# A second feed-forward product by seven products instead of eight, in three parts of its inner dimension

## The chip, the cores and the metric

The kernel runs on one core of a Trainium2 chip. The metric is the time of one execution on the device, in microseconds (us); a kernel is run several times and the median counts. One further execution is taken with the hardware profiler, and the rows below come from it. Its engines are TensorE (PE; its weight loads are PEld), VectorE (DVE), ScalarE (ACT), GpSimd (POOL) and SyncE (SP), whose queue issues nearly all DMAs.

## The reference

One layer of a streaming encoder on `x` of 2048 x 1024, all in float32. The mixer sub-layer (convolution, gated recurrence and chunked attention side by side) comes first and is not touched. What matters here is the second sub-layer:

```python
h = x * (1.0 + sc2) + sh2
gt, up = jnp.split(h @ w_ffn_in[l], 2, axis=-1)      # 2048 x 1024 @ 1024 x 5632
y = (jax.nn.silu(gt) * up) @ w_ffn_out[l]            # 2048 x 2816 @ 2816 x 1024
x = layer_norm(ALPHA * x + (1.0 + g2) * y, ln2_g[l], ln2_b[l])
```

The second feed-forward product is the one with `w_ffn_out`, of inner dimension 2816, which is 22 slabs of 128.

## The kernel before

The program's instructions are emitted in program order with priorities (`shifted(tc, -BOOST)` takes a block ahead by 2000), and the framework's own timeline then fixes the order of each engine's queue. It takes work far ahead where buffers are free. Each queue is worked off in order.

Every float32 product is made of three passes. An operand is split into a rounded high part and a low rest (`split_hl`, L828: a cast on ScalarE, L829, and a subtraction on VectorE, L830), and `PASSES` multiplies high by high, high by low and low by high. One matmul takes a stationary block of 128 x 128 and a moving one of 128 x 512.

The first feed-forward product (`ffn_in`, L943) already works by a seven-product scheme. Its inner dimension of 1024 is taken in two halves of `NK` = 4 slabs, its tokens in two rounds `g` of 1024, each in two blocks of 512. `load_ops` (L868) loads the moving operands of a round, seven combinations of four slabs, from DRAM into 28 pairs of tiles (`oph`, `opl`) through raw buffers of the tag `h2`, six deep. `load_fi` (L904) loads the weights of slab `f` into `fraw`, forms the seven stationary combinations with four GpSimd operations (L930, L931, L933, L937) and splits each into `fhi` and `flo`. The loop over `f` (22 slabs) then makes 84 matmuls per slab in four PSUM banks (L953), adds on VectorE while they drain (L958), applies SiLU, multiplies (L986) and writes the slab's 1024 tokens to DRAM (`actd`). Weights of slab `f+1` are loaded while `f` is multiplied.

The second product (`ffn_out`, L1022) is plain. It takes the 1024 output columns in two halves `dh` of 512. For each it loads 22 weight slabs as moving operands (`wo`, raw buffers `wraw`, five deep) and the rows `ga`, `ba` (the first norm's scale and shift times ALPHA) and `g2`. Tokens go in blocks of four tiles of 128, the last four in two blocks of two. For each block the activations come back from DRAM (`araw`), are split (`ahi`, `alo`) and multiplied (`mul`, L1095): 22 slabs x 3 passes into one bank per tile. `fetch` loads the residual row (L1043), scales it on ScalarE (L1045) and on GpSimd (L1046, L1047); `evac` multiplies the bank by `g2` (L1116), adds (L1117) and takes the statistics (L1111). The first half's rows wait in DRAM (`zh`); in the second half `norm_out` (L1050) normalizes a tile (L1065 to L1067) and stores it. The very last tile is multiplied in two column halves of 256 and ends in four steps on VectorE (L1060, L1062).

Of the kernel before, what the change touches and what calls it, by code (L numbers as in the profile page):

```python
# [38 lines left out]
N_H2 = 6  # L39
LN2 = 0.6931471805599453  # L40
# [792 lines left out]
def ffn_open(tc, env):  # L833
    pf = env["pf"] = ExitStack()
    env["p1"] = pf.enter_context(tc.tile_pool(name="p1", bufs=1, side="right", reuse_waits="tile"))
    st = env["st_es"] = ExitStack()
    env["st"] = st.enter_context(tc.tile_pool(name="st", bufs=1, side="right", reuse_waits="tile"))
    env["actd"] = [tc.dram_tile([P, NG * 2 * Q], F32, name=f"actd{f}") for f in range(NF)]
    env["ops"] = load_ops(tc, env, 0, range(2))
# [64 lines left out]
def load_fi(tc, env, f, first=False):  # L904
    nc, pw = tc.nc, env["pw"]
    ops = []
# [14 lines left out]

    def op(src):
        hi = pw.tile([P, NK, P], F32R, name="fhi", tag="fhi", bufs=N_WOP)
        lo = pw.tile([P, NK, P], F32R, name="flo", tag="flo", bufs=N_WOP)
        split_hl(nc, src, hi, lo)
        ops.append((hi, lo))
# [15 lines left out]

def ffn_in(tc, env, g, f, w, ops):  # L943
    nc, pw = tc.nc, env["pw"]

    def bank():
        k = "pj" if f % 2 else "pm"
        return env[k].tile([P, Q], F32, name="pi", tag=k)

    def prod(out, n, first):  # L950
        for idx in range(NK):
            for i, (a, c) in enumerate(PASSES):
                nc.tensor.matmul(out=out, lhsT=w[n][a][:, idx, :], rhs=ops[n, idx][c],  # L953
                                 start=first and idx == 0 and i == 0, stop=idx == NK - 1 and i == 2,
                                 skip_group_check=not first)
# [31 lines left out]
    nc.sync.dma_start(out=env["actd"][f][:, g * 2 * Q:(g + 1) * 2 * Q], in_=s.rearrange("p a b -> p (a b)"))  # L987


def ffn_phase(tc, env):  # L990
# [11 lines left out]
    for g in range(NG):  # L1002
        for f in range(NF):
# [18 lines left out]
def ffn_out(tc, env, p2):  # L1022
    nc = tc.nc
    rows, w_fo, out = (env[k] for k in ("rows", "w_fo", "out"))
    epsc, NQ, pw = env["epsc"], env["NQ"], env["pw"]
    NT = NQ * NB
    zh = tc.dram_tile([NT, P, 512], F32, name="zh")
    st2 = p2.tile([P, NT, 2, 6], F32, name="st2")
    st4 = p2.tile([P, 4, 6], F32, name="st4")
    mv = p2.tile([P, NT, 2], F32, name="mv2")  # L1030
    rs = p2.tile([P, NT, 2], F32, name="rs2")

    def row_half(i, dh, tag, bufs=1):
        t = p2.tile([P, 512], F32, name="row", tag=tag, bufs=bufs)
        nc.sync.dma_start(out=t, in_=rows[i, dh * 512:dh * 512 + 512].partition_broadcast(P))
        return t

    def residual(t, dh, ga, ba):
        q, tt = t // NB, t % NB
        sc, nb = env["norms"][q]  # L1040
        ry = pw.tile([P, 2, 512], F32, name="res", tag="fu", bufs=N_U)
        r = ry[:, 0]
        nc.sync.dma_start(out=r.rearrange("p (b c) -> p b c", b=2),  # L1043
                          in_=env["zall"][q * 4 + 2 * dh:q * 4 + 2 * dh + 2, :, tt, :].rearrange("b p c -> p b c"))
        nc.scalar.activation(out=r, in_=r, func=AF.Identity, scale=sc[:, tt:tt + 1], bias=nb[:, tt:tt + 1])  # L1045
        nc.gpsimd.tensor_tensor(out=r, in0=r, in1=ga, op=ALU.mult)  # L1046
        nc.gpsimd.tensor_tensor(out=r, in0=r, in1=ba, op=ALU.add)  # L1047
        return r, ry[:, 1]

    def norm_out(t, z0, z1, lg, lb):  # L1050
        nc.vector.bn_aggr(out=mv[:, t, :], in_=st4 if t == NT - 1 else st2[:, t])
        nc.scalar.activation(out=rs[:, t, 0:1], in_=mv[:, t, 1:2], func=AF.Sqrt, bias=epsc[:, 0:1])
        nc.vector.reciprocal(out=rs[:, t, 0:1], in_=rs[:, t, 0:1])
        last = t == NT - 1
        if not last:
            nc.vector.scalar_tensor_tensor(out=rs[:, t, 1:2], in0=mv[:, t, 0:1], scalar=-1.0, in1=rs[:, t, 0:1],
                                           op0=ALU.mult, op1=ALU.mult)
        for dh, z in enumerate((z0, z1)):
            if last:
                nc.vector.scalar_tensor_tensor(out=z, in0=z, scalar=mv[:, t, 0:1], in1=lg[dh],  # L1060
                                               op0=ALU.subtract, op1=ALU.mult)
                nc.vector.scalar_tensor_tensor(out=z, in0=z, scalar=rs[:, t, 0:1], in1=lb[dh],  # L1062
                                               op0=ALU.mult, op1=ALU.add)
            else:
                nc.scalar.activation(out=z, in_=z, func=AF.Identity, scale=rs[:, t, 0:1], bias=rs[:, t, 1:2])  # L1065
                nc.vector.tensor_tensor(out=z, in0=z, in1=lg[dh], op=ALU.mult)
                nc.vector.tensor_tensor(out=z, in0=z, in1=lb[dh], op=ALU.add)  # L1067
            nc.sync.dma_start(out=out[t * P:(t + 1) * P, dh * 512:dh * 512 + 512], in_=z)

    lg = lb = None  # L1070
    for dh in range(2):
        blocks = [range(4 * i, 4 * i + 4) for i in range(4)]
        if dh:
            blocks = blocks[:3] + [range(12, 14), range(14, 16)]
        with shifted(tc, -BOOST):
            wo = [load_op(tc, env, w_fo[f * P:(f + 1) * P, dh * 512:dh * 512 + 512], f % NK, p2, "wraw", 5)
                  for f in range(NF)]
            ga, ba, g2 = (row_half(i, dh, f"row{i}") for i in (R_LN1G, R_LN1B, R_G2))
            nc.sync.dma_start(out=g2, in_=env["g2d"][:, dh * 512:dh * 512 + 512])
            for r in (ga, ba):  # L1080
                nc.vector.tensor_scalar(out=r, in0=r, scalar1=ALPHA, scalar2=None, op0=ALU.mult)
            if dh:
                lg = [row_half(R_LN2G, i, "rowlg", 2) for i in range(2)]
                lb = [row_half(R_LN2B, i, "rowlb", 2) for i in range(2)]
        for bi, ts in enumerate(blocks):
            k = "pj" if bi % 2 else "pm"
            n = len(ts)
            pts = [env[k].tile([P, 512], F32, name="po", tag=k) for _ in ts]
            tail = ts[-1] == NT - 1 and n == 2
            zr, parts = {}, {}  # L1090

            def mul(f, j, c=slice(0, 512)):
# [122 lines left out]
```

## Time and profile before

| | us |
|---|---|
| median of 3 runs | 2602.72 |
| lowest and highest | 2598.47, 2602.81 |
| the profiled execution | 2589.91 |
| its span, first to last instruction | 2588.2 |
| first product, first to last matmul start | 1227.0 to 2094.7 |
| second product, first to last matmul start | 2086.0 to 2580.2 |

The two products overlap by some 8 us, since the first matmuls of the second one stand between the last ones of the first. A busy TensorE counts from the start of a matmul to its modelled end, and matmuls overlap; how many are started in a stretch tells more than the mean duration.

### The profile page before, as it was taken

Reading aid. Unit: us, or ns where it says so; the run is one execution under the profiler, and the core shown is the slowest. Engines: PE = TensorE matmul, PEld = TensorE weight load, DVE = VectorE, ACT = ScalarE, POOL = GpSimd, SP = SyncE. Lnnn points to the kernel's source line nnn. Section 1 sums busy time; section 2 is a strip of 40 time slices with the busy share of each in tenths; the row PEclk is TensorE's granted clock in tenths of the full one; section 3 lists DMA queues with packets and bytes.
Section 4 is the critical chain, followed back from the end, with each engine's and each line's share of the span. In section 5 each row is a group of like instructions: output and inputs, shape, how many; then the busy total and the mean of one; then the engine's idle time right before and its main releaser. Section 6 shows DMA issues by size and latency. Waiting matters only on the chain.

```text
span 2588.2 us, 36360 instructions
## 1 busy us (share of the span) xinstructions
PE 2457.8 (95%) x13274; PEld 2078.5 (80%) x13274; DVE 1656.1 (64%) x2917; ACT 997.2 (39%) x1920; POOL 665.7 (26%) x571
## 2 busy tenths in 40 slices
PE   6888899999999999987999999999999999999998
PEld 5766799879977898876878788888888888888887
DVE  7987696669557785666655555765445474364666
ACT  2444444354244433544323333433333352242333
POOL 3433112200152112510333332332322211111121
PEclk8997999999999999988999999999999999999999
DMA  9676667663755645547333332442222274454544
GB/s 354 212 236 187 186 197 264 201 180 128 241 183 172 205 164 184 191 135 259 102 117 119 118 130 90 164 142 91 74 82 90 74 244 142 130 182 134 161 147 142
DMA packets 202691, 423.99 MB, mean 164 GB/s; under 512 B 20240, under 2 KB 69008, under 8 KB 202512
## 3 DMA queue, kind: packets, MB, share of 16 engines
q1 hardware_dynamic: 202352, 421.15, 49.8%
q8 instruction: 104, 1.70, 0.3%
q14 instruction: 75, 0.61, 0.1%
q0 software_dynamic: 160, 0.52, 0.1%
HBM read 317.78 MB, written 95.42 MB: 160 GB/s over the span
## 4 chain that ended last, share of the span: by engine, by line
PE 78%; DVE 10%; DMA 6%; issue 3%; ACT 2%; POOL 1%; SPq 0%; DVEq 0%; POOLq 0%; ACTq 0%
PE pi L953 31%; PE po L1095 17%; PE pjt L270 11%; PE pjt L321 9%; PE lp L513 2%; DVE cacc L377 2%; PE sc L625 1%; PE tp L661 1%; PE tp L648 1%; DMA whl<-wki 1%; DMA whl<-wko 1%; PE lp L533 1%; DMA xst<-zall 1%; DMA opraw<-srcd 1%; DMA xb<-in_x_dram 1%
## 5 line engine op out<-in xcount | busy, mean ns | idle before, releaser
L953 PE MATMUL pi<-oph,fhi 128*128 128x512 f32 x1232 | 484.1, 393 | 17.8 <-ACT fhi L829 11.9
L953 PE MATMUL pi<-opl,fhi 128*128 128x512 f32 x1232 | 483.7, 393 | 0.0
L953 PE MATMUL pi<-oph,flo 128*128 128x512 f32 x1232 | 478.9, 394 | 0.0
L270 PE MATMUL pjt<-hh,whl 128*128 128x512 f32 x1184 | 402.5, 411 | 16.2 <-DMA whl<-wki 6.4
L953 PEld LDWEIGHTS pi<-oph,fhi 128*128 128x128 f32 x1232 | 232.4, 189 | 70.2 <-ACT fhi L829 12.1
L829 ACT CAST fhi<-fraw 128x512 fp32r<-128x512 f32 x220 | 136.2, 621 | 392.3 <-PE pi L953 376.6
L270 PEld LDWEIGHTS pjt<-hh,whl 128*128 128x128 f32 x1184 | 227.4, 194 | 66.4 <-DMA whl<-wki 6.0
L958 DVE TENSOR_TENSOR fu<-fu,pi 128x512 f32<-128x512 f32 x176 | 120.8, 686 | 245.8 <-PE pi L953 245.1
L953 PEld LDWEIGHTS pi<-opl,fhi 128*128 128x128 f32 x1232 | 232.5, 189 | 52.3
L1095 PE MATMUL po<-oph,alo 128*128 128x512 f32 (+1 forms) x702 | 273.9, 390 | 0.0
L1095 PE MATMUL po<-oph,ahi 128*128 128x512 f32 (+1 forms) x702 | 270.1, 385 | 3.1 <-DVE res L1116 3.1
L1095 PE MATMUL po<-opl,ahi 128*128 128x512 f32 (+1 forms) x702 | 272.6, 388 | 0.0
L953 PEld LDWEIGHTS pi<-oph,flo 128*128 128x128 f32 x1232 | 232.3, 189 | 49.5 <-DVE flo L830 0.2
L830 DVE TENSOR_TENSOR alo<-araw,ahi 128x512 fp32r<-128x512 f32 x172 | 148.5, 871 | 190.9 <-ACT ahi L829 174.3
L270 PE MATMUL pjt<-hl,whl 128*128 128x512 f32 x592 | 243.0, 411 | 0.0
L321 PE MATMUL pjt<-whl,yh 128*128 128x256 f32 x1024 | 196.7, 288 | 15.5 <-DMA whl<-wko 12.0
L830 DVE TENSOR_TENSOR flo<-fraw,fhi 128x512 fp32r<-128x512 f32 x220 | 159.5, 742 | 70.9 <-ACT fhi L829 70.8
L377 DVE SCALAR_TENSOR_TENSOR cacc<-u,cs,cacc 128x512 f32<-128x512 f32 x240 | 195.3, 843 | 0.2
L829 ACT CAST ahi<-araw 128x512 fp32r<-128x512 f32 x172 | 104.9, 618 | 222.3 <-PE po L1095 208.0
L321 PEld LDWEIGHTS pjt<-whl,yh 128*128 128x128 f32 x1024 | 164.1, 194 | 17.7 <-DVE yl L231 7.9
L930 POOL TENSOR_TENSOR ft<-fraw 128x512 f32<-128x512 f32 x43 | 59.9, 1392 | 450.6 <-DMA fraw<-in_w_fi_dram 433.5
L1095 PEld LDWEIGHTS po<-oph,ahi 128*128 128x128 f32 x702 | 132.4, 189 | 31.7 <-DVE res L1116 3.3
(257 smaller groups left out, 4539.1 us busy)
## 6 DMA issues: line engine op xcount, KB each, us to landing
whl<-wki SPq DMA_DIRECT2D x156, 512.0 KB, 3.8
fraw<-in_w_fi_dram SPq DMA_DIRECT2D x86, 512.0 KB, 3.7
araw<-actd SPq DMA_DIRECT2D x154, 256.0 KB, 3.4
wki<-whl SPq DMA_DIRECT2D x52, 512.0 KB, 4.3
whl<-wko SPq DMA_DIRECT2D x48, 512.0 KB, 3.5
actd<-fs SPq DMA_DIRECT2D x44, 512.0 KB, 3.3
xb<-in_w_ada_dram SPq DMA_DIRECT2D x64, 256.0 KB, 4.7
opraw<-srcd SPq DMA_DIRECT2D x56, 256.0 KB, 5.0
```

Source lines behind the costliest of these rows:

```text
L270: nc.tensor.matmul(out=ps[j], lhsT=w[kt // 2][a][:, kt % 2, j * P:(j + 1) * P], rhs=hts[kt][c], start=(kt == 0 and n == 0), stop=(kt == KT ...
L321: nc.tensor.matmul(out=ps[tt // 2][:, tt % 2, :], lhsT=lhs[2 * kp + k][c][:, tt * P:(tt + 1) * P], rhs=w[kp][a][:, k, :], start=(ko == 0 a ...
L377: nc.vector.scalar_tensor_tensor(out=ac, in0=us[j][:, t:t + Q], scalar=col(wc + t), in1=ac, op0=ALU.mult, op1=ALU.add)
L513: nc.tensor.matmul(out=lp[0:n, c, :], lhsT=ddf[:, c * P:c * P + n], rhs=d4[:, c, :, :], start=True, stop=True)
L533: nc.tensor.matmul(out=lp[:, c, :], lhsT=K[:, 2 * i + c, :], rhs=M[:, 2 * i + c, :], start=True, stop=True)
L625: nc.tensor.matmul(out=sc[:, 0:n + x], lhsT=qs[hd][ph][:, i * P:(i + 1) * P], rhs=kt_[:, o - x0:o - x0 + n + x], start=ph == 0, stop=ph == 1)
L829: nc.scalar.copy(out=hi, in_=src)
L830: nc.vector.tensor_tensor(out=lo, in0=src, in1=hi.bitcast(F32), op=ALU.subtract)
L930: e.tensor_tensor(out=t1, in0=w12, in1=w11, op=ALU.subtract)
L953: nc.tensor.matmul(out=out, lhsT=w[n][a][:, idx, :], rhs=ops[n, idx][c], start=first and idx == 0 and i == 0, stop=idx == NK - 1 and i == ...
L958: nc.vector.tensor_tensor(out=out, in0=a, in1=b, op=ALU.add)
L1095: nc.tensor.matmul(out=pts[j][:, c], lhsT=a[x][:, j * P:(j + 1) * P], rhs=wo[f][y][:, c], start=f == 0 and m == 0, stop=f == NF - 1 and m ...
```

## The change

The second product goes by the same seven-product scheme as the first. Two token tiles of 128 are the halves of the stationary side, two column halves of 512 those of the moving side, and the inner slabs are taken in pairs: 11 pairs. Seven operands of all 11 pairs don't fit in the 28 pairs of tiles, so the pairs are taken in three parts of 4, 3 and 4 (`PARTS`). Each part goes over all tokens in 8 units of two tiles. Between parts the two 1024-wide rows of a unit go to DRAM (`zp`) and come back.

- `wo_part`, called 11 times in the second round of the first product: loads a pair of weight slabs in four blocks, multiplies them by `g2` (four GpSimd operations), forms the combinations (four more) and writes seven operands to DRAM (`wsrc`). That is 8 GpSimd operations and 11 DMAs of 256 KB each time. It uses the tiles of `st` (`h2`, `h2s`, `xst`).
- `stationary` is the second half of `load_fi`, now for `n` slabs; `products` is the bank and matmul code of `ffn_in`, now for `nk` slabs.
- `ffn_out` is new; `row_half`, `residual`, `norm_out` and the block loop go. `g2` is no longer multiplied there.

```diff
+PARTS = ((0, 4), (4, 3), (7, 4))
...
+def wo_part(tc, env, p):
...
+            nc.sync.dma_start(out=t, in_=env["w_fo"][(2 * p + k) * P:(2 * p + k + 1) * P, h * 512:h * 512 + 512])
+            e.tensor_tensor(out=t, in0=t, in1=env["g2r"][h], op=ALU.mult)
...
+    e.tensor_tensor(out=s1, in0=a21, in1=a22, op=ALU.add)
+    e.tensor_tensor(out=s2, in0=s1, in1=a11, op=ALU.subtract)
+    e.tensor_tensor(out=s3, in0=a11, in1=a21, op=ALU.subtract)
+    e.tensor_tensor(out=s4, in0=a12, in1=s2, op=ALU.subtract)
+    for n, src in enumerate((a11, s2, s3, a12, s1, a22, s4)):
+        nc.sync.dma_start(out=env["wsrc"][p][n], in_=src)
...
+            if g == 1 and f >= 2 and f % 2 == 0:
+                wo_part(tc, env, f // 2 - 1)
+            if g == 1 and f == NF - 1:
+                wo_part(tc, env, NF // 2 - 1)
...
+    def load_ops(part):
+        p0, n = PARTS[part]
+        return {(m, i): load_op(tc, env, env["wsrc"][p0 + i][m], i, p2, "wraw", 4)
+                for m in range(7) for i in range(n)}
+
+    def load_a(part, u):
...
+        a = [pw.tile([P, NK, 2 * P], F32, name="araw", tag="fraw", bufs=N_RAW) for _ in range(2)]
...
+        return stationary(tc, env, a[0][:, 0:n, 0:P], a[1][:, 0:n, 0:P], a[0][:, 0:n, P:], a[1][:, 0:n, P:], t1, t2)
+
+    def load_z(part, t, ga, ba):
+        r = pw.tile([P, 2, 512], F32, name="zr", tag="fu", bufs=N_U)
+        rf = r.rearrange("p a c -> p (a c)")
+        if part:
+            nc.sync.dma_start(out=rf, in_=zp[t])
+            return r
...
+        nc.scalar.activation(out=rf, in_=rf, func=AF.Identity, scale=sc[:, tt:tt + 1], bias=nb[:, tt:tt + 1])
+        nc.vector.tensor_tensor(out=rf, in0=rf, in1=ga, op=ALU.mult)
+        nc.gpsimd.tensor_tensor(out=rf, in0=rf, in1=ba, op=ALU.add)
+        return r
+
+    def close(part, t, r, lg, lb):
...
+        if part < 2:
+            nc.sync.dma_start(out=zp[t], in_=rf)
+            return
...
+        if t < NT - 2:
...
+            nc.scalar.activation(out=rf, in_=rf, func=AF.Identity, scale=sd, bias=nb)
+            nc.vector.tensor_tensor(out=rf, in0=rf, in1=lg, op=ALU.mult)
+            nc.gpsimd.tensor_tensor(out=rf, in0=rf, in1=lb, op=ALU.add)
+            nc.sync.dma_start(out=out[t * P:(t + 1) * P, :], in_=rf)
+            return
+        for c in (slice(512, D), slice(0, 512)):
+            nc.vector.scalar_tensor_tensor(out=rf[:, c], in0=rf[:, c], scalar=mv[:, t, 0:1], in1=lg[:, c],
...
+    def add(o, b, part, t=None, c=0):
         with shifted(tc, -BOOST):
...
+            nc.vector.tensor_tensor(out=o, in0=o, in1=b, op=ALU.add)
+            if part == 2 and t is not None:
+                nc.vector.bn_stats(out=st2[:, t, c, :], in_=o)
+
+    def unit(part, u, w, ops, z):
...
+        ba, bb = bank(), bank()
+        prod(ba, 0, True)
+        prod(bb, 1, True)
+        with shifted(tc, -BOOST):
+            nc.scalar.copy(out=v, in_=ba)
+        add(v, bb, part)
+        with shifted(tc, -BOOST):
+            for o in (y[:, 1], x[:, 1], y[:, 0]):
+                nc.gpsimd.tensor_tensor(out=o, in0=o, in1=v, op=ALU.add)
+        bc = bank()
+        prod(bc, 2, True)
+        add(y[:, 1], bc, part)
+        prod(ba, 3, False)
+        add(x[:, 0], ba, part, t, 0)
+        bd = bank()
+        prod(bd, 4, True)
+        add(y[:, 1], bd, part, t + 1, 1)
+        prod(bc, 5, False)
+        add(x[:, 1], bc, part, t, 1)
+        prod(bd, 6, False)
+        add(y[:, 0], bd, part, t + 1, 0)
...
+    for i, (part, u) in enumerate(steps):
+        if u == 0:
+            with shifted(tc, -BOOST):
...
+                ops = load_ops(part)
+        z = [load_z(part, 2 * u + k, ga, ba) for k in range(2)]
+        cur = w
+        if i + 1 < len(steps):
+            w = load_a(*steps[i + 1])
+        unit(part, u, cur, ops, z)
+        for k in range(2):
+            close(part, 2 * u + k, z[k], lg, lb)
```

The rows of a unit use four buffers (`fu`, two units), its raw activations four (`fraw`), the split weights seven pairs (`fhi`, `flo`), as in the first product.

## Rows read from the trace of the kernel before

**Rows 1.** The page, its first part: busy time of each engine, share, instructions.

```profile
PE 2457.8 (95%) x13274; PEld 2078.5 (80%) x13274; DVE 1656.1 (64%) x2917; ACT 997.2 (39%) x1920; POOL 665.7 (26%) x571
```

**Rows 2.** Windows: stretch, length, busy PE, PEld, DVE, ACT, POOL; PEclk, DMA share, GB/s.

```profile
1650.00:1700.00 50.00, 50.00 (x219) 40.67 (x218) 45.64 (x62) 28.18 (x52) 14.87 (x8) 1.00 0.80 259
...
1800.00:1900.00 100.00, 100.00 (x439) 82.05 (x438) 48.02 (x67) 31.56 (x53) 28.00 (x20) 1.00 0.24 81
...
2100.00:2200.00 100.00, 100.00 (x438) 82.07 (x437) 49.31 (x62) 31.31 (x51) 18.22 (x12) 1.00 0.54 172
2200.00:2300.00 100.00, 100.00 (x438) 82.06 (x437) 51.44 (x67) 32.63 (x53) 24.84 (x16) 1.00 0.50 156
```

**Rows 3.** TensorE's waits from 1250 us on: total us, times, longest.

```profile
PE pi L953 <- DVE fu L958: 5.4, 3, 2.4
PE po L1095 <- DVE res L1116: 3.1, 1, 3.1
```

**Rows 4.** Groups by form, one of the three passes: full and half-width matmuls.

```profile
L1095 PE MATMUL po<-oph,ahi 128*128 128x512 f32 x674 | 261.5, 388 | 0.0
...
L1095 PE MATMUL po<-oph,ahi 128*128 128x256 f32 x28 | 8.6, 306 | 3.1 <-DVE res L1116 3.1
```

**Rows 5.** The chain that ended last, pieces of the stage's beginning and end.

```profile
2086.43 1.60 PE po L1095 x7
2088.03 2.75 PE pi L953 x12
...
2571.17 9.35 PE po L1095 x66
```

**Rows 6.** Groups by form on VectorE, 1227 to 2589 us.

```profile
L830 DVE TENSOR_TENSOR flo<-fraw,fhi 128x512 fp32r<-128x512 f32 x220 | 159.5, 742 | 70.9 <-ACT fhi L829 70.8
...
L986 DVE TENSOR_TENSOR fs<-fs,fu 128x1024 f32<-128x1024 f32 x44 | 53.7, 1220 | 0.0
```

**Rows 7.** A group of GpSimd's weight combinations.

```profile
L933 POOL TENSOR_TENSOR fraw<-fraw 128x512 f32<-128x512 f32 x43 | 69.5, 1616 | 3.0
```

**Rows 8.** Timeline of GpSimd in two stretches: start us, us, operation.

```profile
1664.55 1.69 POOL L937 TENSOR_TENSOR fraw<-fraw,ft 128x512 f32<-128x512 f32 x1 [1.83 <-DVE flo L830]
1666.32 1.62 POOL L931 TENSOR_TENSOR ft<-fraw,ft 128x512 f32<-128x512 f32 x1
...
1907.76 1.30 POOL L930 TENSOR_TENSOR ft<-fraw 128x512 f32<-128x512 f32 x1 [12.38 <-DMA fraw<-in_w_fi_dram]
1909.13 1.63 POOL L933 TENSOR_TENSOR fraw<-fraw 128x512 f32<-128x512 f32 x1
```

**Rows 9.** Timeline of VectorE in the same stretches.

```profile
1664.40 4.09 DVE L830 TENSOR_TENSOR opl<-opraw,oph 128x512 fp32r<-128x512 f32 x3
...
1907.94 0.69 DVE L958 TENSOR_TENSOR fu<-fu,pi 128x512 f32<-128x512 f32 x1 [1.39 <-PE pi L953]
1908.54 1.06 DVE L830 TENSOR_TENSOR flo<-fraw,fhi 128x512 fp32r<-128x512 f32 x1
1911.16 0.69 DVE L830 TENSOR_TENSOR flo<-fraw,fhi 128x512 fp32r<-128x512 f32 x1 [1.55 <-ACT fhi L829]
```

**Rows 10.** Waits of all engines, 1225 to 2589 us: total us, times, longest.

```profile
ACT fhi L829 <- PE pi L953: 515.6, 277, 6.6
POOL ft L930 <- DMA fraw<-in_w_fi_dram: 433.5, 38, 14.1
...
POOL fraw L937 <- DVE flo L830: 80.3, 41, 16.6
```

**Rows 11.** SP's issues of operand loads (start, us), and the DMA table's line for them.

```profile
1655.67 18.58 SPq L862 DMA_DIRECT2D opraw<-srcd  x17
...
opraw<-srcd SPq DMA_DIRECT2D x56, 256.0 KB, 5.0
```

**Rows 12.** Windows of 3 us at the last block's wait, columns as in rows 2.

```profile
2570.00:2573.00 3.00, 1.83 (x8) 1.84 (x9) 1.96 (x5) 0.00 (x0) 0.00 (x0) 0.60 0.47 175
2573.00:2576.00 3.00, 3.00 (x24) 3.00 (x23) 0.00 (x0) 0.00 (x0) 0.00 (x0) 0.84 0.00 0
```

More of the change, by code (lines that the diff above doesn't have):

```diff
@@ L905, in load_fi @@
     nc, pw = tc.nc, env["pw"]
-    ops = []
     if first:
@@ L940, in load_fi, with products, bank, prod @@
     return ops
+def wo_part(tc, env, p):
+    nc, st = tc.nc, env["st"]
+    e = nc.gpsimd
+    if p == 0:
+        env["g2r"] = [st.tile([P, 512], F32, name="g2r", tag="xst", bufs=3) for _ in range(2)]
+        for h, t in enumerate(env["g2r"]):
+            nc.sync.dma_start(out=t, in_=env["g2d"][:, h * 512:h * 512 + 512])
+    a = {}
+    for k in range(2):
+        for h in range(2):
+            t = a[k, h] = st.tile([P, 512], F32, name="wos", tag="h2", bufs=N_H2)
+            nc.sync.dma_start(out=t, in_=env["w_fo"][(2 * p + k) * P:(2 * p + k + 1) * P, h * 512:h * 512 + 512])
+            e.tensor_tensor(out=t, in0=t, in1=env["g2r"][h], op=ALU.mult)
+    a11, a21, a12, a22 = a[0, 0], a[0, 1], a[1, 0], a[1, 1]
+    s1, s2, s3, s4 = (st.tile([P, 512], F32, name="wos", tag="h2s", bufs=4) for _ in range(4))
+    e.tensor_tensor(out=s1, in0=a21, in1=a22, op=ALU.add)
[4 more added lines that the diff above has]
+        nc.sync.dma_start(out=env["wsrc"][p][n], in_=src)
+def products(tc, env, i, w, ops, nk):
+    nc = tc.nc
+    def bank():
+        k = "pj" if i % 2 else "pm"
+        return env[k].tile([P, Q], F32, name="pi", tag=k)
+    def prod(out, n, first):
+        for idx in range(nk):
+            for j, (a, c) in enumerate(PASSES):
+                nc.tensor.matmul(out=out, lhsT=w[n][a][:, idx, :], rhs=ops[n, idx][c],
+                                 start=first and idx == 0 and j == 0, stop=idx == nk - 1 and j == 2,
+                                 skip_group_check=not first)
+    return bank, prod
 def ffn_in(tc, env, g, f, w, ops):
     nc, pw = tc.nc, env["pw"]
[L946 to L955, printed above, removed]
+    bank, prod = products(tc, env, f, w, ops, NK)
     def add(out, a, b):
@@ L1023, in ffn_out @@
     nc = tc.nc
[L1024 removed]
+    rows, out = env["rows"], env["out"]
     epsc, NQ, pw = env["epsc"], env["NQ"], env["pw"]
     NT = NQ * NB
[L1027 to L1029 removed]
+    zp = [tc.dram_tile([P, D], F32, name=f"zp{t}") for t in range(NT)]
     mv = p2.tile([P, NT, 2], F32, name="mv2")
     rs = p2.tile([P, NT, 2], F32, name="rs2")
[L1033 to L1036 removed]
@@ L1045, in residual @@
[L1045 to L1056, printed above, removed]
-                                           op0=ALU.mult, op1=ALU.mult)
[L1058 to L1068, printed above, removed]
@@ new lines, in ffn_out @@
+    lg = lb = ga = ba = None
+    nu = NT // 2
+    steps = [(part, u) for part in range(3) for u in range(nu)]
+    w = load_a(0, 0)
+    for i, (part, u) in enumerate(steps):
+        if u == 0:
+            with shifted(tc, -BOOST):
+                if part == 0:
+                    ga, ba = row(R_LN1G), row(R_LN1B)
+                    for r in (ga, ba):
+                        nc.vector.tensor_scalar(out=r, in0=r, scalar1=ALPHA, scalar2=None, op0=ALU.mult)
+                if part == 2:
+                    lg, lb = row(R_LN2G), row(R_LN2B)
+                ops = load_ops(part)
[4 more added lines that the diff above has]
+        unit(part, u, cur, ops, z)
+        for k in range(2):
+            close(part, 2 * u + k, z[k], lg, lb)
```

134 lines of the change are left out of this document (36 added, 98 removed).

## The prediction

> **What bounds the kernel now.** The page's busy shares come first: TensorE holds 95% of the span, VectorE 64%, GpSimd 26% [rows 1]. Busy PE alone proves little, so the second view is the table by stretches: in the stage that is rewritten TensorE is busy in all of 2100 to 2300, at the full granted clock (2.4 GHz), and starts 438 matmuls in each 100 us, one per 0.2283 us (84 in a second-product unit: 19.18 us); VectorE is half busy, GpSimd a fifth [rows 2]. The third view is TensorE's waits: after 1250 us there are 8.5 us of them in all, 3.1 of these in the last block [rows 3]. So the stage is bound by the number of matmuls; a matmul removed is worth 0.2283 us, so long as everything else keeps under TensorE's pace. The question is what that "so long as" costs.
>
> **1. Matmuls.** Before, 2 halves x 16 tiles x 22 slabs x 3 passes = 2112, the last tile's second 66 split into two of 256 columns [rows 4]: 2046 full ones x 0.2283 = 467.1, and 132 halves at 9.35/66 = 0.1417 us [rows 5] = 18.7; with the 3.1 us wait, 488.9. The chain agrees: 2086.43 to 2580.51, less the two interleaved pieces of the first product, is 488.6 [rows 5]. After, 7 products x 3 passes x (4+3+4) x 8 units = 1848 x 0.2283 = 421.9. Gain 67.0, the ceiling.
>
> **2. The port in the steady units.** An uncontended 512-wide GpSimd add takes 1.30 us, the next starts 0.07 later; the timelines then show it and VectorE taking turns. A VectorE subtraction with both inputs in SBUF that starts inside a GpSimd add takes 1.06 us instead of the 0.69 of its neighbour, ending 0.54 after that add; the GpSimd add behind it takes 1.63. Three `opl` subtractions beside two adds need 4.09 us [rows 8, 9]. An add from PSUM meanwhile keeps its 0.69. So two-SBUF VectorE work and GpSimd work exclude each other; an add holds the port for 1.16 us (the second one ends that long after the subtraction does, 1910.76 less 1909.60) and a subtraction for about 0.55. The Trainium skill is of two minds. Its GPSIMD Engine Reference, § Specifications, names instructions with two SBUF inputs among those that contend, as the rows do; Advanced Engine Details and Errata, § VectorE Performance Modes, lets only the two-port modes block GpSimd and gives `tensor_tensor` none, by which the 13 us below would be nothing and the sum 39 instead of 26. The rows here decide for the first.
> A full unit of part 0 or 2 gives GpSimd seven 512-wide adds (four for the next weights, three of `v`) and two 1024-wide ones. No row shows a 1024-wide one: between 2.3 us (two port times) and 3.2 (two contended ones); I take 2 x 1.30, the least that one alone takes, twice. It meets seven subtractions, each costing it 0.33, and two 1024-wide VectorE multiplies, 0.9 each (their row is 1.22, next start 0.09 earlier [rows 6]). Sum 7 x 1.37 + 2 x 2.67 + 7 x 0.33 + 2 x 0.9 = 19.0 us, against TensorE's 19.18: level. VectorE, at 0.60 a slot [rows 9], does in part 2 seven subtractions, six PSUM adds, four statistics, two multiplies of 1.13 and about 0.8 of small work: 13.3, and about nine waits of 0.7 for the port: 19.6, just over. In part 0 it is 10.1 + 6.3. Part 1 is lighter in all (three slabs, no wide adds): GpSimd about 10 of 14.4 us. Units next to a part's border have no wide adds either, so six units in each of parts 0 and 2 are heavy. With a queue this full, some waits reach TensorE: I take 0.6 us per unit in part 0 and 1.5 in part 2: 4 + 9 = 13 us. Bounds: 0, as in the first product's second round, where GpSimd is 28% busy (1800 to 1900 [rows 2]) and TensorE never waits, and 59 (rival B). I am nearer to the first, since the sums come out level with TensorE and not above.
>
> **3. The three operand loads.** Each part needs 7 x n operand pairs (28, 21, 28), loaded, cast and subtracted while the last unit before still uses the slots. Before has one like it, at 1650 to 1700: VectorE 45.6 of 50 us busy, DMA share 0.80 at 259 GB/s, and no wait on TensorE [rows 2, 3]. Its cover was six raw buffers and little GpSimd work: 17 issues in 18.58 us, 1.09 us per operand, landing in 5.0 [rows 11]. Four buffers stretch that to 1.64. Into part 0: last first-product unit and first new unit hold, in port time, 16.5 (weights for the next unit, the SiLU product, two rows of `z`) and 18.9 (a full unit: 7 x 1.16 + 2 x 2.4 + 7 x 0.55 + 2 x 1.08), and 28 x 0.55 = 15.4: 50.8 in 38.4 us, 12 late. Into part 1: two light units of 9.8 and 21 x 0.55, 31.2 in 33.6, 17 raws past the prefetched four at 1.64 = 28 us before the last is needed at 32.9: I take 2. Into part 2: two units of 12.0 and 15.4, 39.3 in 33.6, 6 late by the port; by bytes, 28 operands of 0.26 MB and two units' own 2.9 and 3.1 MB make 13.3 MB, 41 us at 259/0.80 GB/s, 7 late; the buffers give 6. Together I take 9. Sum 23 us; bounds 0 (the load of before) and 40 (each cause adds to the others). Waits of this size also lower the clock: after the 3.1 us wait the granted clock is 0.60 and 0.84 over the next two 3 us stretches, part of each at the lower level of 1.2 GHz [rows 12], about 1.3 us lost; three times 4 us, rounded for late restarts: 4.
>
> **4. What is hidden, and its cover.** `wo_part` adds 88 GpSimd operations to the second round of the first product, 13 us per two units that already hold 11 of 38 us, and 121 DMAs on SP's queue, in order before the weight loads. TensorE's 100% covers them; GpSimd mostly waits for those loads there, and ACT waits for TensorE [rows 10]. If a store stuck in SP's queue held a weight load for longer than its unit of slack, the whole lateness would show. Partial rows add 2 MB per unit, in and out: with operands 3 MB per 19.18 us = 157 GB/s against 156 to 172 now [rows 2]. In part 1 it is 2.75 MB in 14.4 us, 191, still under 259. A row's reload two units ahead waits for its store; four row buffers leave some 8 us. ACT, at 31% in the stage [rows 2], gets one copy and two row scalings per unit. Cost 0; if that cover goes, the late row delays `y`'s add, then the bank of product 5.
>
> **5. Tail.** After the last matmul, before: 256-wide add, add, statistics, then four 512-wide steps (L1116, L1117, L1109, L1060, L1062), the out store. After: one 512-wide add and statistics less the multiply, but the neighbour tile's closing stands on VectorE as well: +1 us, from 0 to +2.
>
> **Sum.** 67 - 13 - 23 - 4 - 1 = 26 us gained. The profiled execution took 2589.91 (span 2588.2 and 1.7 around it), 12.8 below the median of the runs, 2602.72; I take the gain off each: 2564 for a profile like that one, 2577 for the median. A difference within 0.2%, 5 us, is no difference that a measurement of this kernel can tell.
>
> **Rivals.** A: port and loads stay covered, as at 1650 to 1700. For it: the sums of step 2 lie level with TensorE, and late work can be taken ahead in part 1; against: a full port has no slack and [rows 8, 9] show the exclusion. Then only byte-limited lateness (7), clock (1) and tail (1) remain: gain 58, 2545. Chance 0.2.
> B, slower: GpSimd becomes the bound. The adds of `v` stand in its in-order queue among weight adds that wait for VectorE's subtractions (80.3 us over 41 units now, 2 us each [rows 10]); `y`'s add waits for it, VectorE's queue waits behind that add, and product 5 waits for its bank. A unit would take GpSimd's own 14.9 us, 6 of VectorE's port time and those 2: 22.9, 3.7 over TensorE, in all 16 units of parts 0 and 2: 59 us; with 23 + 4 + 1 it is 20 us slower, 2622. It turns slower from 2.8 us lost per unit on. Against it: order and buffers give a product's length of slack, and part of the 2 us overlaps. Chance 0.18.
> C: the loads cost the 40 of the bound, and 6 for the clock: 67 - 13 - 40 - 6 - 1 = 7 gained, 2596, hardly told from nothing. Four buffers and the common DMA queue speak for it, prefetch against. Chance 0.14.
> That the count of matmuls doesn't fall can be excluded from the loops; that another order of instructions costs something elsewhere I leave in the range.
>
> **Numbers.** Forecast 0.48, nearly all of it faster by over 5 us; A all faster; C a half; B slower. Faster 0.48 x 0.96 + 0.2 + 0.07 = 0.73, less 0.04 for a loss that I don't foresee: 0.69. Same: 0.02 of the forecast, 0.06 of C and 0.03 beside: 0.11. Slower: B and what is left of the others, 0.20. The range goes from A's 2545 with a little cut off, 2548, to 2614, which leaves out the outer half of B.
>
> **What would show it.** Right: 1848 matmuls in the stage; TensorE's waits some 40 us after 2086, a third or more of it in the first units of parts 0 and 2, named by `opl`, `oph` or the raw loads; GpSimd over 85% busy in parts 0 and 2 and half so in part 1; units of 19.5 to 21 us there. Subtractions' mean well above 742 ns [rows 6], GpSimd's 512-wide adds near their contended 1616 [rows 7]. Wrong if units keep 19.2 us with GpSimd that full (A), if they take 23 (B), or if waits stand before the partial rows or the weight loads of the second round.

## The result, and the profile after

The changed kernel takes 2635.36 us in the median of 4 runs against 2602.76 us before: ratio 1.0122, 95% interval 1.0098 to 1.0146. It is 33 us slower, outside the range that was forecast and on the other side. The experiments ran later: e1 to e8 on one chip, where the kernel before took 2591.22 and 2592.42, and e9 to e11 on another, where it took 2592.80 and the changed kernel (e11) 2629.99 (ratio 1.0147, 1.0119 to 1.0174). Ratios are to the kernel before on the same chip. Where a run of e1 to e8 is set against e11, or e9 and e10 against e8, two chips are compared, which the kernel before ties together to about 1.6 us.

The page's first part, after (compare [rows 1]):

```profile
span 2636.0 us, 36091 instructions
...
PE 2435.9 (92%) x12944; PEld 2040.8 (77%) x12944; DVE 1832.8 (70%) x2989; ACT 1000.4 (38%) x1937; POOL 1036.3 (39%) x793
```

TensorE lost work, as meant: 330 matmuls fewer. But the span grew by 47.8 us, and GpSimd's busy time by 371. Where, the windows of the changed kernel tell (columns as in [rows 2]; the number in brackets after PE is the matmuls started):

```profile
1700.00:1900.00 200.00, 177.39 (x735) 140.67 (x734) 122.67 (x119) 48.73 (x89) 185.77 (x123) 0.96 0.70 231
1900.00:2120.00 220.00, 220.00 (x963) 180.52 (x962) 111.39 (x152) 72.23 (x123) 64.31 (x47) 1.00 0.25 86
2140.00:2180.00 40.00, 29.25 (x107) 19.71 (x106) 40.00 (x35) 15.81 (x27) 27.85 (x14) 0.96 0.59 179
2180.00:2320.00 140.00, 129.05 (x538) 103.20 (x537) 110.59 (x107) 45.06 (x70) 101.37 (x55) 0.96 0.51 169
2320.00:2360.00 40.00, 33.93 (x134) 26.72 (x133) 29.29 (x41) 15.55 (x30) 17.64 (x15) 0.91 0.74 237
2360.00:2440.00 80.00, 80.00 (x351) 65.66 (x350) 57.49 (x78) 27.04 (x53) 47.92 (x38) 1.00 0.72 218
2440.00:2480.00 40.00, 34.11 (x135) 27.09 (x134) 36.90 (x45) 17.71 (x32) 22.75 (x15) 0.91 0.79 253
2480.00:2620.00 140.00, 130.33 (x539) 103.99 (x538) 123.84 (x166) 49.34 (x79) 98.18 (x54) 0.96 0.40 130
```

One matmul per 0.2283 us would be 876 in the first line; 735 were started, so 141 x 0.2283 = 32.2 us are missing. By the same sum the others lose: 15.6 us where part 0 begins (2140 to 2180), 17.2 in its full units, 9.4 where part 1 begins (2320 to 2360), nothing in part 1 itself (351 of 350), 9.2 where part 2 begins (2440 to 2480), 17.0 in its full units. The second product loses 68 us, all of the 67 that the missing matmuls were worth. Its length, here and in the experiments, is taken from the first copy of `v` to the start of the last high-by-high matmul, 487.3 us:

```profile
L985 PE MATMUL pi<-oph,fhi x1848: 387/392/796, 1236.6 to 2625.8; 128*128 128x512 f32 x185
...
L1152 ACT COPY v<-pi x24: 563/578/583, 2138.5 to 2610.1; 128x512 f32<-128x512 f32 x24
```

The chain gave 488.6 for the whole product before [rows 5]. The first product loses 32 on top. The tail adds 1.6 (the span ends 9.3 us after TensorE's last work, 7.7 before). The remaining 10 us of the two profiles lie ahead of the first product, in the mixer, whose code is the same: 1236.6 against 1227.0 at the first matmul. The profiles of the experiments, with the same mixer, have it anywhere from 1216.9 (e5) to 1242.5 (e4).

Not all of this loss is standing still. By the column of busy PE, TensorE stands for 43 of the 68 us in the second product and for 22.6 of the 32 in the first. In the rest it is busy but starts fewer matmuls, and there the granted clock is below 1.00, as in this stretch of part 2 with 73 starts where 88 fit:

```profile
2560.00:2580.00 20.00, 19.80 (x73) 15.97 (x74) 18.54 (x25) 5.90 (x10) 16.60 (x10) 0.84 0.55 170
```

So up to 25 us of the second product's loss go with the lower clock that follows the waits.

TensorE's waits from 1200 us on name `fu` in the first product and `zr` and `opl` in the second. The one for `fhi` is the start of the first product (11.9 us before); from 1250 us on they come to 71 us, against 8.5 before [rows 3].

```profile
PE pi L985 <- DVE zr L1139: 26.8, 11, 3.9
PE pi L985 <- ACT fu L1006: 15.0, 7, 4.7
PE pi L985 <- DVE fu L998: 13.1, 11, 2.1
PE pi L985 <- ACT fhi L830: 13.0, 1, 13.0
PE pi L985 <- DVE opl L831: 11.7, 14, 1.8
```

**The first loss** is plain in GpSimd's timeline at its start (start, us):

```profile
1711.21 1.72 POOL L969 TENSOR_TENSOR wos<-wos 128x512 f32<-128x512 f32 x1
1712.90 1.74 POOL L964 TENSOR_TENSOR wos<-wos,g2r 128x512 f32<-128x512 f32 x1
1714.60 1.75 POOL L970 TENSOR_TENSOR wos<-wos 128x512 f32<-128x512 f32 x1
1716.31 1.74 POOL L939 TENSOR_TENSOR ft<-fraw 128x512 f32<-128x512 f32 x1
1718.01 1.29 POOL L964 TENSOR_TENSOR wos<-wos,g2r 128x512 f32<-128x512 f32 x1
1719.26 1.29 POOL L942 TENSOR_TENSOR fraw<-fraw 128x512 f32<-128x512 f32 x1
```

There is no gap between these operations: `wo_part`'s (`wos`) fill the queue, and the weight combinations of the first product (`ft`, `fraw`) stand between them. The 11 calls, written for 20 slabs, all run in 185 us, 1695 to 1880. ScalarE's timeline shows who pays, with its wait in brackets:

```profile
1768.83 0.62 ACT L830 CAST fhi<-fraw 128x512 fp32r<-128x512 f32 x1 [10.44 <-POOL fraw L946]
...
1793.68 0.62 ACT L830 CAST fhi<-fraw 128x512 fp32r<-128x512 f32 x1 [15.50 <-POOL fraw L946]
...
1795.77 0.57 ACT L1006 COPY fu<-pi 128x512 f32<-128x512 f32 x1
```

A cast waits 15.5 us for GpSimd, and behind it in ScalarE's queue stands the copy to `fu` that empties a bank of TensorE. In this stretch TensorE waits 15.0 us for such copies and 7.6 for VectorE's additions to `fu`.

**The second loss** is told by the groups by form, 2140 to 2636 (columns as in [rows 6]):

```profile
L1156 POOL TENSOR_TENSOR zr<-zr,v 128x512 f32<-128x512 f32 x72 | 117.7, 1662 | 25.7 <-DVE v L1139 25.7
L831 DVE TENSOR_TENSOR flo<-araw,fhi 128x512 fp32r<-128x512 f32 x76 | 85.5, 1131 | 11.7 <-ACT fhi L830 11.7
L1139 DVE TENSOR_TENSOR zr<-zr,pi 128x512 f32<-128x512 f32 x120 | 80.2, 676 | 26.0 <-POOL zr L1156 21.2 <-PE pi L985 4.8
L831 DVE TENSOR_TENSOR opl<-opraw,oph 128x512 fp32r<-128x512 f32 x64 | 73.4, 1174 | 11.7 <-ACT oph L830 11.7
L831 DVE TENSOR_TENSOR flo<-at,fhi 128x512 fp32r<-128x512 f32 x30 | 42.4, 1414 | 0.0
L1110 POOL TENSOR_TENSOR zr<-zr,row 128x1024 f32<-128x1024 f32 x15 | 40.4, 2695 | 25.2 <-DVE zr L1109 25.2
```

Subtractions with two inputs in SBUF take 1131 to 1414 ns where 690 is the uncontended time, additions from PSUM keep 676, and each of the two engines also stands still for the other: GpSimd's adds of `v` wait 25.7 us for VectorE, VectorE's adds from the banks 21.2 for GpSimd.

The port isn't the only thing that makes `zr` late. In part 0's full units (2180 to 2320) TensorE waits 9.7 us for `zr`, in four waits. The longest, 3.71 us, is the end of this chain (timelines of four engines, in order of time):

```profile
2286.64 1.25 ACT L1108 ACTIVATE zr<-zr,nrm 128x1024 f32<-128x1024 f32 x1 [6.23 <-DMA zr<-zall]
2287.92 1.22 DVE L1109 TENSOR_TENSOR zr<-zr,row 128x1024 f32<-128x1024 f32 x1 [5.85 <-ACT zr L1108]
2289.23 2.39 POOL L1110 TENSOR_TENSOR zr<-zr,row 128x1024 f32<-128x1024 f32 x1 [8.30 <-DVE zr L1109]
2291.58 5.64 POOL L1156 TENSOR_TENSOR zr<-zr,v 128x512 f32<-128x512 f32 x3
2293.76 0.68 DVE L1139 TENSOR_TENSOR zr<-zr,pi 128x512 f32<-128x512 f32 x1
2294.49 0.80 PE L985 MATMUL pi<-oph,fhi 128*128 128x512 f32 x1 [3.71 <-DVE zr L1139]
```

The residual row comes late: its load is issued at 2282.40, after the store at 2277.70 of a row two units back, from the ring of four row buffers. ScalarE, VectorE and GpSimd wait for it in turn, GpSimd idle for 8.3 us. The wait of 1.74 us at 2250 has the same origin; ahead of the other two stand long subtractions (1.7 to 2.5 us).

### The profile page after: what moved, and what is told of

It is laid out like the page before. It is cut to its first block, busy times and chain, and to the rows that moved or that the text cites. A ratio compares the mean times of both kernels' runs of the same rounds, so it can differ in the third digit from the quotient of the medians.

```text
span 2636.0 us, 36091 instructions
## 1 busy us (share of the span) xinstructions
PE 2435.9 (92%) x12944; PEld 2040.8 (77%) x12944; DVE 1832.8 (70%) x2989; ACT 1000.4 (38%) x1937; POOL 1036.3 (39%) x793
## 4 chain that ended last, share of the span: by engine, by line
PE 58%; DVE 16%; DMA 13%; issue 6%; POOL 5%; ACT 2%; SPq 1%; DVEq 0%; POOLq 0%; ACTq 0%
PE pi L985 30%; PE pjt L271 10%; PE pjt L322 8%; DVE flo L831 3%; PE lp L514 2%; DVE opl L831 2%; DVE cacc L378 2%; POOL wos L964 2%; PE sc L626 1%; PE tp L662 1%; DMA xb<-in_w_ada_dram 1%; PE tp L649 1%; DMA ft<-in_xT_dram 1%; DMA whl<-wki 1%; DVE zr L1139 1%
## 5 line engine op out<-in xcount | busy, mean ns | idle before, releaser
L985 PE MATMUL pi<-oph,fhi 128*128 128x512 f32 x1848 | 737.4, 400 | 72.7 <-DVE zr L1139 26.8
L985 PE MATMUL pi<-opl,fhi 128*128 128x512 f32 x1848 | 735.2, 398 | 11.7 <-DVE opl L831 11.7
L985 PE MATMUL pi<-oph,flo 128*128 128x512 f32 x1848 | 724.4, 397 | 0.2 <-DVE flo L831 0.2
L985 PEld LDWEIGHTS pi<-oph,fhi 128*128 128x128 f32 x1848 | 353.5, 191 | 164.5 <-DVE zr L1139 33.3
L985 PEld LDWEIGHTS pi<-opl,fhi 128*128 128x128 f32 x1848 | 354.1, 192 | 95.2 <-DVE opl L831 18.0
L271 PE MATMUL pjt<-hh,whl 128*128 128x512 f32 x1184 | 402.7, 411 | 20.3 <-DMA whl<-wki 10.5
L322 PEld LDWEIGHTS pjt<-whl,yh 128*128 128x128 f32 x1024 | 164.4, 194 | 15.6 <-DVE yl L232 7.7
L322 PE MATMUL pjt<-whl,hh 128*128 128x256 f32 x768 | 152.1, 291 | 1.2 <-POOL whl L232 0.6
L322 PE MATMUL pjt<-whl,yl 128*128 128x256 f32 x512 | 146.5, 288 | 0.0
L831 DVE TENSOR_TENSOR opl<-opraw,oph 128x512 fp32r<-128x512 f32 x133 | 124.1, 964 | 23.7 <-ACT oph L830 23.5
L494 POOL TENSOR_TENSOR tmp<-recB 128x512 f32<-128x512 f32 x96 | 124.3, 1321 | 40.3 <-PE ms L552 12.3
L831 DVE TENSOR_TENSOR flo<-araw,fhi 128x512 fp32r<-128x512 f32 (+1 forms) x120 | 125.1, 1047 | 17.5 <-ACT fhi L830 17.5
```

The lines of the kernel that those rows point to most:

```text
L271: nc.tensor.matmul(out=ps[j], lhsT=w[kt // 2][a][:, kt % 2, j * P:(j + 1) * P], rhs=hts[kt][c], start=(kt == 0 and n == 0), stop=(kt == KT ...
L322: nc.tensor.matmul(out=ps[tt // 2][:, tt % 2, :], lhsT=lhs[2 * kp + k][c][:, tt * P:(tt + 1) * P], rhs=w[kp][a][:, k, :], start=(ko == 0 a ...
L494: nc.gpsimd.tensor_tensor(out=dd, in0=Bv, in1=r.unsqueeze(2).broadcast_to([P, nb, 2, s]), op=ALU.subtract)
L831: nc.vector.tensor_tensor(out=lo, in0=src, in1=hi.bitcast(F32), op=ALU.subtract)
```

## The experiments

**e1** puts the calls of `wo_part` alone into the kernel before.

```diff
+            if g == 1 and f >= 2 and f % 2 == 0:
+                wo_part(tc, env, f // 2 - 1)
+            if g == 1 and f == NF - 1:
+                wo_part(tc, env, NF // 2 - 1)
```

> The kernel before with the calls of wo_part alone added; the second product stays plain, nothing reads wsrc. Theory (the 11 calls run as one burst in which GpSimd is full, the weight combinations of the first product stand behind it, TensorE waits): about 32 us slower than before, 2635, all of it in some 200 us of the first product's second round, and the second product unchanged at about 489. Rival (the first product's loss comes with the new order of the whole program, or from DMA): less than 10 us slower.

2628.08 us against 2591.22, ratio 1.0140 (1.0116 to 1.0163): 37 us slower, as much as the whole change. Its windows:

```profile
1700.00:1900.00 200.00, 180.55 (x746) 142.91 (x744) 123.86 (x121) 49.31 (x91) 183.13 (x121) 0.97 0.71 235
1900.00:2120.00 220.00, 220.00 (x963) 180.52 (x962) 114.28 (x159) 71.92 (x122) 56.88 (x41) 1.00 0.28 92
2130.00:2330.00 200.00, 200.00 (x875) 164.11 (x874) 103.38 (x131) 65.67 (x108) 45.98 (x30) 1.00 0.52 163
```

130 matmuls, 30 us, are missing in the same 200 us, and none afterwards. So the part of the change that leaves the second product alone already costs what the whole change does.

**e2** spreads the same work: before each weight load of `wo_part` one column of its tile is written from the slab before.

```diff
             t = a[k, h] = st.tile([P, 512], F32, name="wos", tag="h2", bufs=N_H2)
+            nc.vector.tensor_copy(out=t[:, 0:1], in_=env["tick"][:, 0, 0:1])
...
                       in_=s.rearrange("p a b -> p (a b)"))
+    env["tick"] = s
```

> The changed kernel, with each call of wo_part held until the slab before it is multiplied: a one-column copy from that slab's result is put ahead of each weight load. Same work, spread over 22 slabs instead of 9. Theory (burst): 25 to 32 us faster than the changed kernel, 2603 to 2610, TensorE at 88 matmuls per 20 us all through the second round. Rival (the work itself costs, by port or DMA, wherever it stands): less than 10 us faster, 2625 or more.

2627.74 us, ratio 1.0138 (1.0115 to 1.0162): by the time, the theory would be refuted. The windows say otherwise:

```profile
1700.00:2080.00 380.00, 380.00 (x1662) 311.81 (x1661) 228.09 (x296) 115.79 (x198) 231.31 (x159) 1.00 0.48 157
2080.00:2140.00 60.00, 28.92 (x97) 20.84 (x96) 35.76 (x38) 19.77 (x30) 33.08 (x20) 0.66 0.66 215
```

TensorE is full through the round with the same GpSimd work in it. Then 166 matmuls, 38 us, are missing at once; the longest wait is one:

```profile
PE pi L986 <- ACT oph L830: 23.3, 1, 23.3
```

The last call now ends with the first product, and the raw buffers of part 0, which lie where `st` lay, can be filled only after it. The burst had paid for an early release.

**e5** keeps the hold and places the calls so that the last is at slab 18:

```diff
-            if g == 1 and f >= 2 and f % 2 == 0:
-                wo_part(tc, env, f // 2 - 1)
-            if g == 1 and f == NF - 1:
-                wo_part(tc, env, NF // 2 - 1)
+            for p in range(NF // 2):
+                if g == 1 and f == 2 + 8 * p // 5:
+                    wo_part(tc, env, p)
```

> As e2 (each call of wo_part held by the slab before), but eight calls per thirteen slabs or so, the last at slab 18, three slabs before the second product needs the buffers of st. Theory (the burst cost 32 us; e2 gave them back because its last call ended with the first product and part 0's loads then waited for st's buffers): TensorE at its full pace through the second round, no long wait at the start of part 0, time level with the kernel before, -5 to +6 us. Rival (part 0's loads are late anyway): still 20 us or more slower than before.

2598.92 us against 2592.42, ratio 1.0020 (1.0002 to 1.0037): 6.5 us over the kernel before, just past the upper end of the expectation, and 31 under the changed kernel (e11: 2629.99). Windows of e5: the two stretches of the round, and the start of part 0.

```profile
1680.00:1880.00 200.00, 199.68 (x873) 163.52 (x872) 125.77 (x165) 59.75 (x104) 128.42 (x88) 1.00 0.50 169
1880.00:2070.00 190.00, 187.30 (x815) 152.55 (x814) 113.42 (x149) 57.64 (x103) 117.28 (x81) 1.00 0.53 174
2086.00:2126.00 40.00, 31.29 (x118) 21.92 (x117) 40.00 (x36) 18.69 (x31) 25.43 (x13) 0.96 0.55 172
```

The round loses 5 us instead of 32, and part 0 begins as in the changed kernel. Its second product takes 485.2 us, measured as above, against 487.3: the first loss is settled, the second untouched.

**e3** takes the wide GpSimd additions away.

```diff
-        nc.gpsimd.tensor_tensor(out=rf, in0=rf, in1=ba, op=ALU.add)
...
-            nc.gpsimd.tensor_tensor(out=rf, in0=rf, in1=lb, op=ALU.add)
```

> The changed kernel without the two 1024-wide GpSimd additions per unit of parts 0 and 2 (the rows ba and lb are not added, so the residual and the result lack them); nothing else. Theory (in full units GpSimd and the port are full): the steady loss of parts 0 and 2, about 37 us, falls by 20 to 30: 2605 to 2615. Rival (the loss is latency: the adds of v stand in GpSimd's queue behind weight adds, VectorE and TensorE wait in turn): less than 10 us faster.

2602.24 us, ratio 1.0037 (1.0021 to 1.0053): 28 us under e11, as the theory said. Instructions of the tile `pi` and the copy to `v`, with first and last start:

```profile
L985 PE MATMUL pi<-oph,fhi x1848: 388/392/794, 1233.9 to 2593.9; 128*128 128x512 f32 x185
...
L1150 ACT COPY v<-pi x24: 562/578/585, 2137.8 to 2578.8; 128x512 f32<-128x512 f32 x24
```

The second product takes 456.1 us, 31 less, for 29 recorded operations of 2.6 to 2.7 us (15 of 2695 ns, 14 of 2634), some 0.4 of their length. But each addition is also a step on the way of a row, between its load or its normalizing and its use or store. So e3 doesn't separate GpSimd's time and the port from rows that are ready earlier.

**e4** gives the operands six raw buffers instead of four.

```diff
-        return {(m, i): load_op(tc, env, env["wsrc"][p0 + i][m], i, p2, "wraw", 4)
+        return {(m, i): load_op(tc, env, env["wsrc"][p0 + i][m], i, p2, "wraw", 6)
```

> The changed kernel with six raw buffers for the operands instead of four. Theory (the loads into the parts are late by VectorE and the port): 0 to 5 us faster. Rival (late by the four buffers): 10 to 20 us faster, most of it in the first units of parts 0 and 2.

2627.57 us, ratio 1.0139 (1.0108 to 1.0170), not to be told from the changed kernel's; its second product takes 483.1 us, 4 less. Its waits show why: those for `opl` are gone (0.9 us), those for `zr` have grown from 26.8.

```profile
PE pi L985 <- DVE zr L1139: 37.5, 21, 4.5
...
PE pi L985 <- DVE opl L831: 0.9, 2, 0.7
```

By missing matmuls, the beginnings of the three parts lose 23 us instead of 34, and the full units 41 instead of 35.

**e6 and e7** start from e5 and take the additions of `v` to VectorE. In e6 `v` lies in PSUM, in e7 in SBUF:

```diff
-        add(v, bb, part)
         with shifted(tc, -BOOST):
-            for o in (y[:, 1], x[:, 1], y[:, 0]):
-                nc.gpsimd.tensor_tensor(out=o, in0=o, in1=v, op=ALU.add)
+            nc.vector.tensor_tensor(out=bb, in0=v, in1=bb, op=ALU.add)
+        for o in (y[:, 1], x[:, 1], y[:, 0]):
+            add(o, bb, part)
```

> e5 with the three additions of v taken from GpSimd to VectorE, and v left in its PSUM bank, so that they don't use the port: GpSimd 4 us shorter per unit, VectorE 1.8 us longer. Theory (port): 10 to 25 us faster than e5. Rival (VectorE is the bound in part 2): no faster, or slower.

> e5 with the three additions of v on VectorE, but v in SBUF, so that they take the port for 0.55 us each. It differs from e6 in the port alone. Theory (port): 5 us or more behind e6. Rival (what matters is that the chain from v to TensorE's bank leaves GpSimd's queue): level with e6 within 3 us.

e6 takes 2584.02 us, ratio 0.9966 (0.9954 to 0.9978), 15 less than e5; e7 2591.65, ratio 0.9991 (0.9977 to 1.0005), 7 less. Their second products take 464.7 and 476.8 us. GpSimd does the same in both, and VectorE's additions are as many; what differs is where `v` lies, and with it whether they use the port. From 2140 to 2560, first e6's additions to the rows, which all read a bank, then e7's of `v`:

```profile
L1140 DVE TENSOR_TENSOR zr<-zr,pi 128x512 f32<-128x512 f32 x178 | 115.8, 676 | 19.7 <-PE pi L986 15.5 <-DMA zr<-zp 4.0
...
L1140 DVE TENSOR_TENSOR zr<-zr,v 128x512 f32<-128x512 f32 x66 | 57.9, 922 | 1.4 <-DMA zr<-zp 1.3
```

So 7.6 us of e6's gain come from keeping these additions off the port. The other 7.3, which e7 has too, come from taking them off GpSimd; that this is its shorter queue, and not also the port that it holds for less time, isn't shown. This is the point on which two sections of the Trainium skill differ: its GPSIMD Engine Reference, § Specifications, names VectorE instructions with two SBUF inputs among those that contend, and the trace agrees with that page (922 ns against 676, and 7.6 us between e6 and e7), not with the note and the table in Advanced Engine Details and Errata, § VectorE Performance Modes.

**e8** is e6 with part 0's wide addition on VectorE and six raw buffers:

```diff
-        nc.gpsimd.tensor_tensor(out=rf, in0=rf, in1=ba, op=ALU.add)
+        nc.vector.tensor_tensor(out=rf, in0=rf, in1=ba, op=ALU.add)
...
-        return {(m, i): load_op(tc, env, env["wsrc"][p0 + i][m], i, p2, "wraw", 4)
+        return {(m, i): load_op(tc, env, env["wsrc"][p0 + i][m], i, p2, "wraw", 6)
```

> e6 with part 0's wide addition of ba on VectorE too (port 1.1 instead of 2.4 us each) and six raw buffers for the operands. Theory: 5 to 15 us faster than e6, so 15 to 35 faster than the kernel before. Rival (VectorE then bounds part 0): no faster than e6.

2568.77 us, ratio 0.9912 (0.9885 to 0.9940): 15 less than e6, and faster than both kernels. Its second product takes 450.4 us, and part 0 now begins without a loss:

```profile
2080.00:2140.00 60.00, 60.00 (x264) 49.24 (x263) 58.06 (x76) 33.47 (x58) 26.02 (x12) 1.00 0.73 238
2140.00:2280.00 140.00, 130.16 (x539) 103.46 (x538) 116.38 (x151) 55.12 (x88) 40.90 (x26) 0.96 0.58 188
```

264 matmuls in 60 us, where the changed kernel started 107 of 175 in 40. The six raw buffers alone gave 4 us (e4), and e6, with four, still loses 10 us in part 0's first 40; e8 changes the buffers and the wide addition together, so which of the two removed that isn't separated. The full units still lose 17 us of 140, now with GpSimd at 29%.

**e9 and e10** ask what holds e8. e9 issues the reloads of the partial rows from ACT's queue (`nc.scalar.dma_start(out=rf, in_=zp[t])`); e10 takes part 2's wide addition to VectorE too.

> e8 with the reloads of the partial rows (zp) issued from ACT's queue instead of SP's, where a reload that waits for its buffer holds up the activation loads behind it. Theory (SP's order matters in parts 1 and 2): 3 to 10 us faster than e8. Rival (the rows are late by their four buffers, whichever queue waits): within 3 us of e8, or slower, since ACT then stands still.

> e8 with part 2's wide addition of lb on VectorE as well, so that GpSimd keeps the four weight additions only. Theory (in part 2 VectorE has no room: 15 us own work and its port waits of 19): within 4 us of e8. Rival (the port is what binds, as in part 0): 8 to 15 us faster than e8.

e9: 2564.28 us, ratio 0.9896 (0.9865 to 0.9927); e10: 2566.02, 0.9900 (0.9874 to 0.9926). Neither can be told from e8. In both the second product is as long as in e8 (452.0 and 450.9 us), and TensorE's waits for `zr` stay (19.9 and 22.9 us, 18.2 in e8). For e10 that is what the theory said, in part 2 VectorE has no room, though late rows would give the same. For e9 it speaks for the rival, rows late by their four buffers; more buffers for them weren't tried.

**e11** is the changed kernel again, on the chip of e9 and e10.

> The changed kernel on the chip of the other experiments, to compare them with it directly. All theories: 1.2% over the kernel before, 29 to 37 us.

2629.99 us against 2592.80, 37 us slower, at the end of what was expected.

**Where the gains lie.** The loss of the second product, as missing matmuls x 0.2283 us, in the stretches of the changed kernel's windows, laid at the same distance from the first copy of `v` in every profile; part 2's full units here run to the last matmul. The last column is GpSimd's busy share in part 0's full units.

| | part 0 begins | its full units | part 1 begins | part 2 begins | its full units | GpSimd |
|---|---|---|---|---|---|---|
| changed | 15.6 | 17.2 | 9.4 | 9.2 | 17.5 | 72% |
| e5 | 15.8 | 16.7 | 8.0 | 8.0 | 18.0 | 73% |
| e4 | 10.8 | 20.4 | 1.6 | 10.8 | 20.6 | 74% |
| e3 | 7.4 | 12.8 | 2.8 | 8.3 | 1.3 | 51% |
| e7 | 10.5 | 22.0 | 5.5 | 2.8 | 18.2 | 47% |
| e6 | 9.9 | 15.6 | 1.4 | 2.3 | 17.3 | 50% |
| e8 | 0.0 | 16.7 | 0 | 2.6 | 14.0 | 29% |
| e10 | 0.3 | 15.8 | 1.6 | 0.0 | 13.0 | 28% |

What e6 and e8 win lies nearly all where the parts begin. The full units gain little when GpSimd's work goes to VectorE, however idle GpSimd becomes; they gain in e3, where that work is left out and the rows have a step less to go. That the port costs something there too is seen between e7 and e6, 22.0 against 15.6.

## Why the prediction was wrong, by its own steps

- **Step 1, matmuls:** right. 1848 are there, and where nothing waits one starts every 0.228 us (part 1, 351 in 80 us). The 67 us are real and were lost elsewhere.
- **Step 4, what is hidden, is the step that failed.** It set `wo_part` at "13 us per two units that already hold 11 of 38 us", cost 0. The durations were right (1.5 to 1.7 us per operation), the place was not: the schedule takes work as far ahead as buffers allow, and the 11 calls ran at once, 88 operations and the 39 weight combinations among them, in a queue that was full from 1692 to 1884 but for some 3 us. It cost 32 us (e1: 37 by the time, 30 by its windows; e5: 31 back). Even the cover that was named ("GpSimd mostly waits for those loads") was read from waits that the change itself fills. The warning that weight loads would be late was there, but it was looked for in SP's queue, not in GpSimd's. The same step also put the rows at nothing, under a cover of "some 8 us" from four row buffers. That cover goes in part 0's full units, the way the step itself names: two of the four waits there, 5.5 of 9.7 us, end a chain that begins with a late row.
- **Step 2, the port:** 13 us said for the steady units, 34 measured (17.2 and 17.0). The exclusion is real: the subtractions for the next weights take 0.44 to 0.72 us longer than the 690 ns of an uncontended one, where 0.7 was taken for a wait. That it makes the 34 us is not shown. The sum had GpSimd 99% busy and level with TensorE; it is 72% busy in part 0's full units and 70% in part 2's. With its share cut to 50% (e6) and 29% (e8) part 0's full units still lose 15.6 and 16.7 us. Nor is it shown to be rival B's chain through GpSimd's adds of `v`: e6 has none and loses as much, though VectorE has that work then. At 2.7 us per full unit (34.2 us over 12.8 units' worth of matmuls) the size came near B's 3.7, by another way. Late rows are what the traces show beside the port; how the 34 us divide stays open.
- **Step 3, operand loads:** 23 us said, 34 measured (15.6, 9.4, 9.2). That the port and GpSimd's work hold them up is shown by e6, which takes the adds of `v` off both and has 14 us left there. The four buffers have a part too: with six the beginnings lose 11 us less, but the full units then lose 6 more (e4), so that little is won by them alone. Into part 1 it was 9.4 and not 2, and of that 6.1 us are two waits for `zr` and none for `opl`: the adds were late there, not the operands.
- **The clock in step 3:** 4 us said, for three waits; up to 25 us of the second product's loss are matmuls started more slowly after many waits. They are contained in the 34 and 34 above.
- **Step 5, tail:** +1 said, +1.6 measured.
- The sum with the measured terms is 67 - 32 - 34 - 34 - 2 = -35, and the two measurements gave -33 and -37. The terms were read off the profile of the same kernel, so that this agreement tests the bookkeeping and not the causes. The slower side had a chance of 0.20, but rival B put it on GpSimd's queue in the second product alone; the 32 us in the first had no rival.

Still open: what the last 30 us of e8's second product (450.4 against 419, which is 421.9 less the 12 matmuls before the first copy) would need, nearly all of it in the full units of parts 0 and 2. The four row buffers, seen in the waits, and VectorE's load in part 2 are argued from traces and from e9 and e10; no run tests either.

## What to carry to other kernels

Side work that is written into a loop is hidden only if something holds it there: where a schedule may run ahead, look for the buffer or the wait that stops it, and size it as a burst in the queue of its engine. Then ask what its end releases, since pacing it later can make the next stage wait (e2). When two engines exclude each other on a port and also feed each other, a sum of busy times that comes out level with the bound doesn't tell the loss: here neither engine was full and the units were still late. Follow TensorE's wait back to the step that began it, row buffers included, before pricing the port. A PSUM operand in place of an SBUF one takes work off the port; here that was worth as much (7.6 us, e6 against e7) as taking the same work off GpSimd (7.3 us, e7 against e5).

## What was not expected of the hardware

A VectorE operation on one column with two SBUF operands takes 727 ns in the changed kernel, where its counterpart before took 146 (L1056). It does almost no work, so nearly all of that is waiting; that it is for the port is inferred.

```profile
L1123 DVE SCALAR_TENSOR_TENSOR rs<-mv,rs 128x1 f32<-128x1 f32 x14 | 10.2, 727 | 0.3
```

In e2's wait of 23.3 us (2090 to 2114) the granted clock falls: it is 0.50, the lower level of 1.2 GHz, from 2098 to 2134, while TensorE first stands and then runs with gaps, and 0.99, the level of 2.4 GHz, from 2134 to 2140, when it runs without them. At the lower level matmuls that nothing holds start 0.43 us apart (2130 to 2133), at the upper one 0.23. So part of the 38 us lost there is matmuls at the lower clock.
